# Cutting the tokens of a two-layer decoder step at 256 and 320 columns instead of 288 and 288

## The chip, the cores and the metric

The kernel runs on one core of a Trainium2 chip. The metric is the device time of one execution in microseconds, lower is better. Three runs of the kernel before gave a median of 1583.88 us (1583.41 to 1588.03).

## What is computed

One inference step of two transformer layers with a width of 1024, for 576 tokens: a prompt of 512 tokens and eight samples of eight tokens, all with the same weights. In each layer:

```
mod = silu(c) @ w_ada + b_ada            -> shift, scale and gate, twice
h   = x * (1 + scale1) + shift1
proj = h @ w_in                          (22 column blocks of 128)
   retention, 8 heads (q, k, v, gate)    and sliding-window attention, 8 query heads, 2 kv heads
x   = LN1(alpha * x + gate1 * (concat(ret, swa) @ w_out))
h2  = x * (1 + scale2) + shift2
u   = causal depthwise conv3(h2 @ w_up)  (44 column blocks of 128)
x   = LN2(alpha * x + gate2 * ((silu(u_a) * u_b) @ w_down))
```

The prompt shares one set of modulations; each sample has its own. The outputs are x and the new states of retention, window and convolution.

## The kernel before

Activations lie transposed: 128 features on the partitions, the 576 tokens along the free axis, first the 512 of the prompt, then the 64 of the samples. A product with a 128x128 block of weights therefore has the tokens as its moving columns. A PSUM bank takes 512 of them, so every product is made in two parts, called halves, each of `HA` = 288 columns: the first takes tokens 0 to 287, the second tokens 288 to 575, which are 224 of the prompt and the 64 samples.

Accuracy comes from a split: each weight and each activation is held as two float32r parts, a high and a low one, and `gemm` (L363) makes three matmuls per 128x128 block and half: high by high, high by low, low by high (L369, L370, L371). 96 units of eight blocks per layer, two layers, two halves and three matmuls make 9216 matmuls of 288 columns. Each of them loads its own weights.

`gemm2` (L373) makes both halves of a product one after the other, in two PSUM banks; nearly all products go this way. At three places a layer norm stands between two products, and there the halves are taken apart. `halves` (L928) ends a layer's output product: the first halves of the last four blocks, the second half of one of them, then the statistics and the norm of the first half (`LayerNorm.stats`, L445, `norm`, L460, `make_h`, L243), and then the other three second halves. `skewed` (L915) begins the next product: the first halves of four blocks, with the statistics and norm of the second half put in after the first of them, then the four second halves. This happens after the output projection of both layers and after the down projection of the first. After the last down projection `halves` is followed by the statistics of the second half and `y_out` (L1131), which norms and writes the result.

`stats` uses float32 matmuls against a matrix of constants (L448, L449, L451, L452), then VectorE and ScalarE make 1/sqrt of the variance (L454 to L458, the reciprocal is L457). `norm` is a subtract (L463) and a multiply (L464) for each of the eight feature tiles. `make_h` scales and shifts on ScalarE (L249; the samples on VectorE, L252 and L253), rounds to the high part (L254) and subtracts for the low part (L255, on VectorE or GpSimd).

The program states an order of operations; the tile framework's planner, which works with costs of its own, may put an engine's instructions in another order where the data allow it, so the order on VectorE near the norms isn't the order of the lines.

```
o = half * HA
T.matmul(out[:, 0:HA], lhsT=wh, rhs=xh[:, o:o + HA], start=(k == 0), stop=False)
T.matmul(out[:, 0:HA], lhsT=wh, rhs=xl[:, o:o + HA], start=False, stop=False)
T.matmul(out[:, 0:HA], lhsT=wl, rhs=xh[:, o:o + HA], start=False, stop=(k == n - 1))
```

The functions that the change touches, as they stand:

Of the kernel before, what the change touches and what calls it, by code (L numbers as in the profile page):

```python
# [21 lines left out]
NT = 576  # L22
NP = 512
HA = 288
# [38 lines left out]
def ffn_order():  # L63
    """The feed-forward units: the first pair of the next group goes ahead of a group's down products."""
    seq, done = [], 0
    for g, (f0, f1) in enumerate(GROUPS):
        ahead = f1 + (1 if g + 1 < len(GROUPS) else 0)
        seq += [("up", i) for i in range(done, ahead)] + [("down", g)]
        done = ahead
    return seq  # L70


class Weights:
    """The stream of weight units: 8 tiles of 128x128 each, split exactly into two float32r parts."""
# [41 lines left out]
def _body(ctx, tc, nc, a):  # L116
# [56 lines left out]
    class Ada:  # L173
        """Four (or fewer) 512-wide column blocks of silu(c) @ w_ada + b_ada, one row block of w_ada at a time."""
# [68 lines left out]
    def make_h(src, st, k, half, hi, lo, nm):  # L243
        """h of one feature tile and half of the tokens, split into two float32r parts."""
        s_t, t_t = st
        tmp = tok(f"h{nm}", HA)
        o = half * HA
        n = HA if half == 0 else NP - HA
        S.activation(tmp[:, 0:n], src[:, o:o + n], AF.Identity, bias=t_t[:, k, 0:1], scale=s_t[:, k, 0:1])  # L249
        if half == 1:  # L250
            tv = tmp[:, n:HA].rearrange("p (b t) -> p b t", b=8)
            V.tensor_tensor(tv, src[:, NP:NT].rearrange("p (b t) -> p b t", b=8), bc(s_t[:, k, 1:9], 2, 8), ALU.mult)  # L252
            V.tensor_tensor(tv, tv, bc(t_t[:, k, 1:9], 2, 8), ALU.add)  # L253
        S.copy(hi[:, o:o + HA], tmp[:, 0:HA])  # L254
        (G if k in LO_POOL[half] else V).tensor_tensor(lo[:, o:o + HA], tmp[:, 0:HA], hi[:, o:o + HA].bitcast(F32), ALU.subtract)  # L255

# [4 lines left out]
    # the first modulations, then h  # L261
# [48 lines left out]
    # the bias of the sliding window by distance, by head  # L310
# [52 lines left out]
    def gemm(tiles, X, out, half):  # L363
        n = len(tiles)
        o = half * HA
        for k in range(n):
            wh, wl = tiles[k]
            xh, xl = X[k]
            T.matmul(out[:, 0:HA], lhsT=wh, rhs=xh[:, o:o + HA], start=(k == 0), stop=False)  # L369
            T.matmul(out[:, 0:HA], lhsT=wh, rhs=xl[:, o:o + HA], start=False, stop=False)  # L370
            T.matmul(out[:, 0:HA], lhsT=wl, rhs=xh[:, o:o + HA], start=False, stop=(k == n - 1))  # L371
# [32 lines left out]
    class LayerNorm:  # L404
# [7 lines left out]
        def shift_base(self, m, half, base):  # L412
            """Takes the shift off what the layer's product is added to, once the shift is known."""
            if m > 1:
                o = slice(half * HA, half * HA + HA)
                G.tensor_tensor(base[:, o], base[:, o], self.shift[:, o], ALU.subtract)

        def r_done(self, m, half, tail=False):
            """The sums over the features, of values off by the mean of the first 128 features."""
            o = slice(half * HA, half * HA + HA)  # L420
            x, nm = self.X[m], f"{self.nm}{half}"
            if m == 0:
                ps = psum("tr", f"{nm}mean")
                T.matmul(ps[:, 0:HA], lhsT=ones_h, rhs=x[:, o], start=True, stop=True)
                S.copy(self.shift[:, o], ps[:, 0:HA])
# [7 lines left out]
            if m == 7 and tail:  # L433
                t = self.t7 = tok(f"{nm}s{m}", HA)
# [6 lines left out]
            t = tok(f"{nm}s{m}", HA)  # L441
# [3 lines left out]
        def stats(self, half, tail=False):  # L445
            o, nm = slice(half * HA, half * HA + HA), f"{self.nm}{half}"
            pd, pq = psum("tr", f"{nm}pd"), psum("tr", f"{nm}pq")
            T.matmul(pd[:, 0:HA], lhsT=ones_f, rhs=self.sd[:, o], start=True, stop=not tail)  # L448
            T.matmul(pq[:, 0:HA], lhsT=ones_f, rhs=self.sq[:, o], start=True, stop=not tail)  # L449
            if tail:  # L450
                T.matmul(pd[:, 0:HA], lhsT=ones_f, rhs=self.X[7][:, o], start=False, stop=True)  # L451
                T.matmul(pq[:, 0:HA], lhsT=ones_f, rhs=self.t7, start=False, stop=True)  # L452
            t = tok(f"{nm}var", HA)
            S.activation(t, pd[:, 0:HA], AF.Square)  # L454
            V.tensor_tensor(t, pq[:, 0:HA], t, ALU.subtract)
            S.activation(t, t, AF.Sqrt, bias=eps_ln)
            V.reciprocal(self.rs[:, o], t)  # L457
            S.copy(self.sd[:, o], pd[:, 0:HA])  # L458

        def norm(self, k, half, eng=V, both=False):  # L460
            o = slice(half * HA, half * HA + HA)
# [4 lines left out]
    def add_gated(ps, half, g, m, base, out, nm):  # L466
        """out = base + gate * ps."""
        n = HA if half == 0 else NP - HA
        o = half * HA
        V.scalar_tensor_tensor(out[:, o:o + n], ps[:, 0:n], g[:, m, 0:1], base[:, o:o + n], ALU.mult, ALU.add)  # L470
        if half == 1:
            t = small(f"gs_{nm}", 64)
            V.tensor_tensor(t.rearrange("p (b t) -> p b t", b=8), ps[:, n:HA].rearrange("p (b t) -> p b t", b=8),
# [3 lines left out]
    def attention(l):  # L477
# [18 lines left out]
        kv, svk = [None, None], []  # L496

        def it_kv(s):
            t = kv[s] = unit("S", f"{L}kv{s}")

            def evac(half, ps):
                S.copy(t[:, half * HA:half * HA + HA], ps[:, 0:HA])
# [22 lines left out]
        def it_sq(i):  # L525
            t = sq[i] = unit("X", f"{L}sq{i}", w=NP)

            def evac(half, ps):
                if half == 0:
                    S.mul(t[:, 0:HA], ps[:, 0:HA], 0.125)  # L530
                else:
                    S.mul(t[:, HA:NP], ps[:, 0:NP - HA], 0.125)
                    V.tensor_scalar(qsv[:, :, i, :], ps[:, NP - HA:HA].rearrange("p (b t) -> p b t", b=8), 0.125, None,
# [89 lines left out]
        # the sample group's windows: rows (4 batches, 4 heads, 8 tokens)  # L623
# [65 lines left out]
        def it_kq(i, s):  # L689
# [3 lines left out]
            def evac(half, ps):  # L693
                S.mul(raw[:, half * HA:half * HA + HA], ps[:, 0:HA], sc)
# [20 lines left out]
        def it_v(i):  # L715
            t = vT[i] = unit("X", f"{L}vT{i}")

            def evac(half, ps):
                S.copy(t[:, half * HA:half * HA + HA], ps[:, 0:HA])
# [46 lines left out]
        def ret_states(i):  # L766
            """The states of the prompt after each chunk, and the new ones of the sample group."""
# [30 lines left out]
        def ret_out(i):  # L798
# [23 lines left out]
            # normalise each head  # L822
# [15 lines left out]
        def it_gate(i):  # L838
# [3 lines left out]
            def evac(half, ps):  # L842
                o = half * HA
                S.activation(th[:, o:o + HA], ps[:, 0:HA], AF.Tanh, scale=0.5)
                V.scalar_tensor_tensor(gT[:, o:o + HA], th[:, o:o + HA], 1.0, ps[:, 0:HA], ALU.add, ALU.mult)
# [3 lines left out]
        def gate_out(i):  # L849
            """Back to feature rows, and gated."""  # L850
# [64 lines left out]
    def skewed(items, between):  # L915
        """The first half of the tokens of some products, then the second half of the same ones."""
# [11 lines left out]
    def halves(fn, m0, between):  # L928
        """The last products of a layer by halves, the norm of the first half as soon as it can be had."""
# [13 lines left out]
    for l in range(DEPTH):  # L943
# [68 lines left out]
        def up_evac(t, ps, half):  # L1012
            if half == 0:
                S.copy(t[:, 2:2 + HA], ps[:, 0:HA])
            else:
                n = NP - HA
                S.copy(t[:, 2 + HA:514], ps[:, 0:n])  # L1017
                S.copy(t[:, 514:594].rearrange("p (b t) -> p b t", b=8)[:, :, 2:10],
                       ps[:, n:HA].rearrange("p (b t) -> p b t", b=8))
# [111 lines left out]
        def y_out(half):  # L1131
            o = slice(half * HA, half * HA + HA)
            for k in range(KT):
                ln.norm(k, half, G if k in Y_POOL[half] else V, True)
                if k % 2 == 0:
                    y = tok(f"y{k}{half}", 2 * HA)
                y_k = y[:, k % 2 * HA:k % 2 * HA + HA]
# [172 lines left out]
```

## Time and profile before

| | |
|---|---|
| three runs, median | 1583.88 us |
| profiled execution, span from first to last instruction | 1584.1 us |
| TensorE matmul busy | 96% |
| TensorE weight load busy | 87% |
| VectorE busy | 55% |
| ScalarE busy | 41% |
| GpSimd busy | 31% |
| mean granted TensorE clock | 0.975 of full speed |

The profiled execution has no time of its own beside its span; the span is 0.2 us above the median of the runs. The page's second part cuts the span into 40 slices of 39.6 us and gives each engine's busy share in tenths. In the trace a matmul's record is longer than the distance to the next matmul, because matmuls are pipelined: what a matmul costs in a stream is the distance between two starts, not the duration of one record.

### The profile page before, as it was taken

The numbers are of one execution on the slowest core, as the hardware profiler recorded it, in microseconds if no ns is written. First come the engines' busy times: TensorE is split into PE (matmuls) and PEld (weight loads), VectorE is DVE, ScalarE is ACT, GpSimd is POOL, SyncE is SP. The second block draws the span as 40 slices with busy tenths as digits, with TensorE's granted clock in tenths as the row PEclk, the third lists the DMA queues.
The fourth block names the chain that finished last, engine by engine and source line by source line (L and its number), as shares of the span: only waits on it lengthen the run. The fifth ranks groups of instructions, "written<-read, shape, count | busy, mean of one in ns | idle before, by whom it ended". The sixth has DMA issues, their size and how long they took to land. (4 is left out here: it accounts for less than half of the span.)

```text
span 1584.1 us, 28160 instructions
## 1 busy us (share of the span) xinstructions
PE 1513.1 (96%) x11188; PEld 1382.1 (87%) x11188; DVE 875.5 (55%) x1678; ACT 647.3 (41%) x1318; POOL 498.9 (31%) x647
## 2 busy tenths in 40 slices
PE   7899999997999999999999999999899999999995
PEld 3568778897988888999998788979799999999995
DVE  2236356568655234535576656457876534554577
ACT  1224233335743134415436433333485415523543
POOL 2122122155532122213273222115543313322353
PEclk8999999999999999999999999999999999999997
DMA  9545554223355555232222433233122222223211
GB/s 353 182 151 179 173 178 114 78 85 114 107 173 192 200 189 195 81 92 92 87 67 93 128 87 102 75 97 106 61 80 86 91 80 83 81 81 94 83 57 60
DMA packets 95999, 186.37 MB, mean 118 GB/s; under 512 B 30284, under 2 KB 38524, under 8 KB 95740
## 3 DMA queue, kind: packets, MB, share of 16 engines
q1 hardware_dynamic: 80576, 176.52, 34.9%
q10 hardware_dynamic: 15292, 8.06, 1.8%
q8 instruction: 88, 1.44, 0.4%
q14 instruction: 43, 0.35, 0.1%
HBM read 169.56 MB, written 11.83 MB: 115 GB/s over the span
## 5 line engine op out<-in xcount | busy, mean ns | idle before, releaser
L91 ACT CAST wh<-wr 128x1024 fp32r<-128x1024 f32 x192 | 200.5, 1046 | 308.3 <-PE l0wd02b L370 6.5
L96 POOL TENSOR_TENSOR wl<-wr,wh 128x1024 fp32r<-128x1024 f32 x66 | 158.9, 2407 | 494.6 <-ACT wh L91 417.3
L96 DVE TENSOR_TENSOR wl<-wr,wh 128x1024 fp32r<-128x1024 f32 x126 | 157.7, 1252 | 192.1 <-ACT wh L91 159.2
L190 PE MATMUL ada<-wa,cs 128*32 128x512 f32 x384 | 81.9, 619 | 5.1 <-DVE cs L162 5.1
L1023 POOL COPY l0edge<-l0u 128x2 f32<-128x2 f32 x44 | 37.5, 851 | 127.9 <-ACT l0u L1017 127.9
L1031 DVE SCALAR_TENSOR_TENSOR l0c<-l0u,par,l0c 128x592 f32<-128x592 f32 x44 | 48.2, 1097 | 51.0 <-ACT l0c L1030 48.4
L1023 POOL COPY l1edge<-l1u 128x2 f32<-128x2 f32 x44 | 38.3, 871 | 118.1 <-ACT l1u L1017 118.1
L1031 DVE SCALAR_TENSOR_TENSOR l1c<-l1u,par,l1c 128x592 f32<-128x592 f32 x44 | 48.2, 1098 | 46.3 <-ACT l1c L1030 43.6
L1030 ACT ACTIVATE l0c<-l0u,par 128x592 f32<-128x592 f32 x44 | 38.8, 885 | 4.3 <-POOL l0u L1008 1.0
L1030 ACT ACTIVATE l1c<-l1u,par 128x592 f32<-128x592 f32 x44 | 38.8, 884 | 3.3
L1032 DVE SCALAR_TENSOR_TENSOR l1c<-l1u,par,l1c 128x592 f32<-128x592 f32 x44 | 36.6, 834 | 1.4
L1032 DVE SCALAR_TENSOR_TENSOR l0c<-l0u,par,l0c 128x592 f32<-128x592 f32 x44 | 36.6, 834 | 1.4
L190 PEld LDWEIGHTS ada<-wa,cs 128*32 128x32 f32 x384 | 13.0, 109 | 25.3 <-issue 10.9
L394 ACT CAST l1fhi<-l1c 128x512 fp32r<-128x512 f32 (+1 forms) x44 | 16.8, 430 | 37.7 <-DVE l1c L1037 37.7
L704 POOL TENSOR_TENSOR l1sw<-l1sw,c_sin 128x576 f32<-128x576 f32 x8 | 12.9, 1615 | 56.1 <-DMA l1sw<-l1raw 52.0
L704 POOL TENSOR_TENSOR l0sw<-l0sw,c_sin 128x576 f32<-128x576 f32 x8 | 12.4, 1554 | 54.0 <-DMA l0sw<-l0raw 29.2
L394 ACT CAST l0fhi<-l0c 128x512 fp32r<-128x512 f32 (+1 forms) x44 | 16.9, 431 | 28.5 <-DVE l0c L1037 28.1
L1036 ACT ACTIVATE l0c<-l0c 128x592 f32<-128x592 f32 x22 | 15.4, 699 | 25.8 <-DVE l0c L1032 25.8
L395 DVE TENSOR_TENSOR l1flo<-l1c,l1fhi 128x512 fp32r<-128x512 f32 (+1 forms) x44 | 18.2, 455 | 13.0 <-ACT l1fhi L394 13.0
L395 DVE TENSOR_TENSOR l0flo<-l0c,l0fhi 128x512 fp32r<-128x512 f32 (+1 forms) x44 | 18.2, 455 | 11.7 <-ACT l0fhi L394 11.7
L1008 POOL COPY l0u<-l0edge 128x16 f32<-128x16 f32 x44 | 20.8, 484 | 6.8 <-DMA l0edge<-in_hist 6.8
L1008 POOL COPY l1u<-l1edge 128x16 f32<-128x16 f32 x44 | 21.4, 499 | 0.0
(3207 smaller groups left out, 5986.3 us busy)
## 6 DMA issues: line engine op xcount, KB each, us to landing
wr<-in_wst SPq DMA_DIRECT2D x192, 512.0 KB, 3.6
wa<-in_w_ada SPq DMA_DIRECT2D x192, 256.0 KB, 4.3
x<-in_xT SPq DMA_DIRECT2D x8, 288.0 KB, 5.5
l0sw<-l0raw SPq DMA_DIRECT2D x32, 72.0 KB, 2.0
l0xb<-in_xT SPq DMA_DIRECT2D x8, 288.0 KB, 2.8
x_spill<-l0x ACTq DMA_DIRECT2D x8, 288.0 KB, 3.3
l1sw<-l1raw SPq DMA_DIRECT2D x32, 72.0 KB, 2.0
l1xb<-x_spill SPq DMA_DIRECT2D x8, 288.0 KB, 2.7
```

The source lines that it names most:

```text
L91: nc.scalar.copy(hi, raw)
L96: eng.tensor_tensor(lo, raw, hi.bitcast(F32), ALU.subtract)
L190: T.matmul(self.acc[32 * g:32 * (g + 1), :], lhsT=cs[:, k, :], rhs=self.t[k, g], start=(k == 0), stop=(k == KT - 1))
L394: S.copy(hi, src)
L395: V.tensor_tensor(lo, src, hi.bitcast(F32), ALU.subtract)
L704: G.tensor_tensor(sw, sw, sin_t, ALU.mult)
L1008: G.tensor_copy(t[:, 514:594].rearrange("p (b t) -> p b t", b=8)[:, :, 0:2], hist[mt // 11][:, mt % 11, :].rearrange("p (b t) -> p b t", b=8))
L1023: G.tensor_copy(cm[:, 0:2], t[:, 512:514])
L1030: S.activation(c, t[:, 0:592], AF.Identity, bias=w[3], scale=w[0])
L1031: V.scalar_tensor_tensor(c, t[:, 1:593], w[1], c, ALU.mult, ALU.add)
L1032: V.scalar_tensor_tensor(c, t[:, 2:594], w[2], c, ALU.mult, ALU.add)
L1036: S.activation(ca, ca, AF.Silu)
```

## The change

`HA` is replaced by `CUT` = 256 and `HW` = (256, 320). The first half of every product has 256 columns, the second 320: tokens 256 to 575, which are 256 of the prompt and the 64 samples. Whatever is made by halves follows: the moving operands and PSUM columns of `gemm`, the evacuations, the gated add, the sums and statistics of the layer norm, `make_h`, and the tiles and DMAs of `y_out`. The number of instructions of each kind, their order in the program, the buffers and the loads stay. The rest of the diff deletes comments.

```
-HA = 288
+CUT = 256
+HW = (CUT, NT - CUT)
...
     def make_h(src, st, k, half, hi, lo, nm):
         s_t, t_t = st
-        tmp = tok(f"h{nm}", HA)
-        o = half * HA
-        n = HA if half == 0 else NP - HA
+        w = HW[half]
+        tmp = tok(f"h{nm}", w)
+        o = half * CUT
+        n = w if half == 0 else NP - CUT
...
     def gemm(tiles, X, out, half):
         n = len(tiles)
-        o = half * HA
+        o, w = half * CUT, HW[half]
...
-            T.matmul(out[:, 0:HA], lhsT=wh, rhs=xh[:, o:o + HA], start=(k == 0), stop=False)
-            T.matmul(out[:, 0:HA], lhsT=wh, rhs=xl[:, o:o + HA], start=False, stop=False)
-            T.matmul(out[:, 0:HA], lhsT=wl, rhs=xh[:, o:o + HA], start=False, stop=(k == n - 1))
+            T.matmul(out[:, 0:w], lhsT=wh, rhs=xh[:, o:o + w], start=(k == 0), stop=False)
+            T.matmul(out[:, 0:w], lhsT=wh, rhs=xl[:, o:o + w], start=False, stop=False)
+            T.matmul(out[:, 0:w], lhsT=wl, rhs=xh[:, o:o + w], start=False, stop=(k == n - 1))
...
         def y_out(half):
-            o = slice(half * HA, half * HA + HA)
+            o = slice(half * CUT, half * CUT + HW[half])
...
-                    y = tok(f"y{k}{half}", 2 * HA)
-                y_k = y[:, k % 2 * HA:k % 2 * HA + HA]
+                    y = tok(f"y{k}{half}", 2 * HW[half])
+                y_k = y[:, k % 2 * HW[half]:(k % 2 + 1) * HW[half]]
```

## Rows read from the trace of the kernel before

**Rows 1.** The page: busy time by engine, matmul and clock by slice.
```profile
PE 1513.1 (96%) x11188; PEld 1382.1 (87%) x11188; DVE 875.5 (55%) x1678; ACT 647.3 (41%) x1318; POOL 498.9 (31%) x647
...
PE   7899999997999999999999999999899999999995
...
PEclk8999999999999999999999999999999999999997
```

**Rows 2.** The view of cores: span and mean granted clock.
```profile
core 0: 1584.1 us, clock 0.975
```

**Rows 3.** Stretches: length, each engine's busy time (instructions), clock, DMA share, GB/s.
```profile
349.50:403.00 53.50, 45.26 (x298) 42.63 (x297) 40.14 (x80) 31.89 (x67) 27.76 (x31) 0.94 0.33 106
827.50:866.00 38.50, 33.66 (x222) 31.02 (x220) 31.70 (x73) 25.08 (x52) 16.00 (x12) 0.96 0.23 73
1113.00:1166.30 53.30, 45.30 (x302) 43.19 (x301) 40.32 (x80) 32.21 (x68) 27.68 (x31) 0.94 0.20 64
1562.50:1584.10 21.60, 5.02 (x14) 2.77 (x12) 15.65 (x31) 8.67 (x17) 7.72 (x9) 0.57 0.31 109
403.00:806.00 403.00, 402.89 (x3016) 378.28 (x3015) 203.82 (x302) 167.36 (x306) 120.32 (x194) 1.00 0.43 139
1166.30:1520.00 353.70, 353.70 (x2672) 353.70 (x2671) 186.92 (x254) 160.01 (x289) 107.64 (x180) 1.00 0.28 85
268.40:275.00 6.60, 6.11 (x30) 5.61 (x31) 6.29 (x21) 2.07 (x9) 1.41 (x1) 0.50 0.74 198
1142.10:1145.50 3.40, 3.40 (x14) 3.10 (x13) 2.10 (x4) 1.08 (x3) 2.78 (x3) 0.50 0.38 136
```

**Rows 4.** TensorE in order: start, duration; first matmuls of five successive half products.
```profile
1198.08 0.29 PE L369 MATMUL l1up9a<-l1ghi,wh 128*128 128x288 f32 x1
...
1201.24 0.30 PE L369 MATMUL l1up9b<-l1ghi,wh 128*128 128x288 f32 x1
...
1204.44 0.29 PE L369 MATMUL l1up10a<-l1ghi,wh 128*128 128x288 f32 x1
...
1539.81 0.29 PE L369 MATMUL l1wdl<-l1fhi,wh 128*128 128x288 f32 x1
...
1550.87 0.30 PE L369 MATMUL l1wdl<-l1fhi,wh 128*128 128x288 f32 x1
```

**Rows 5.** TensorE in order at half clock: first and last of 18 matmuls.
```profile
270.73 0.44 PE L369 MATMUL l0rv3b<-h0hi,wh 128*128 128x288 f32 x1
...
274.81 0.42 PE L371 MATMUL l0rv3b<-h0hi,wl 128*128 128x288 f32 x1
```

**Rows 6.** Weight loads in order: two that follow each other after a pause.
```profile
1072.82 0.19 PEld L369 LDWEIGHTS l1wo0a<-l1mshi,wh 128*128 128x128 f32 x1 [0.81 <-issue]
1072.92 0.19 PEld L370 LDWEIGHTS l1wo0a<-l1mslo,wh 128*128 128x128 f32 x1
```

**Rows 7.** Groups of weight loads: busy us, mean ns, idle before.
```profile
L370 PEld LDWEIGHTS l1wdl<-l1flo,wh 128*128 128x128 f32 x56 | 10.5, 188 | 0.1
...
L813 PEld LDWEIGHTS l1o<-l1vk,l1sct 128*128 128x128 f32 x64 | 7.5, 191 | 0.1
```

**Rows 8.** TensorE in order: a run of matmuls with 64 columns.
```profile
1013.21 2.00 PE L813 MATMUL l1o<-l1vk,l1sct 128*128 128x64 f32 x16
```

**Rows 9.** TensorE's waits: tile, line, releaser, us in total, times, longest.
```profile
PE l0a1pd L448 <- DVE l0asd L440: 4.0, 1, 4.0
PE l1a1pd L448 <- DVE l1asd L440: 3.9, 1, 3.9
...
PE l1b1pd L448 <- POOL l1bsd L440: 3.1, 1, 3.1
```

**Rows 10.** VectorE in order near the second layer's first norm.
```profile
1145.75 1.94 DVE L457 RECIPROCAL l1ars<-l1a1var 128x288 f32<-128x288 f32 x1
...
1151.83 0.45 DVE L464 TENSOR_TENSOR l1x<-l1x,l1ars 128x288 f32<-128x288 f32 x1
...
1155.01 0.21 DVE L253 TENSOR_TENSOR h1g<-h1g,st_1t 128x64 f32<-128x64 f32 x1
...
1156.66 0.83 DVE L255 TENSOR_TENSOR l1glo<-h1g,l1ghi 128x288 fp32r<-128x288 f32 x2 [0.32 <-ACT l1ghi L254]
```

**Rows 11.** TensorE in order, same place: statistics, and the first matmul after.
```profile
1141.15 0.75 PE L448 MATMUL l1a1pd<-l1asd,ones_f 128*128 128x288 f32 x2 [3.91 <-DVE l1asd L440]
...
1166.28 0.29 PE L369 MATMUL l1up4a<-l1ghi,wh 128*128 128x288 f32 x1
```

**Rows 12.** TensorE's last instructions.
```profile
1562.90 0.29 PE L371 MATMUL l1wdl<-l1fhi,wl 128*128 128x288 f32 x1
1566.32 1.33 PE L448 MATMUL l1b1pd<-l1bsd,ones_f 128*128 128x288 f32 x2 [3.13 <-POOL l1bsd L440]
1567.44 1.17 PE L449 MATMUL l1b1pq<-l1bsq,ones_f 128*128 128x288 f32 x2
1568.40 1.29 PE L451 MATMUL l1b1pd<-l1x,ones_f 128*128 128x288 f32 x2
```

More of the change, by code (lines that the diff above doesn't have):

```diff
@@ L245, in make_h @@
         s_t, t_t = st
-        tmp = tok(f"h{nm}", HA)
-        o = half * HA
-        n = HA if half == 0 else NP - HA
+        w = HW[half]
+        tmp = tok(f"h{nm}", w)
+        o = half * CUT
+        n = w if half == 0 else NP - CUT
         S.activation(tmp[:, 0:n], src[:, o:o + n], AF.Identity, bias=t_t[:, k, 0:1], scale=s_t[:, k, 0:1])
         if half == 1:
-            tv = tmp[:, n:HA].rearrange("p (b t) -> p b t", b=8)
+            tv = tmp[:, n:w].rearrange("p (b t) -> p b t", b=8)
             V.tensor_tensor(tv, src[:, NP:NT].rearrange("p (b t) -> p b t", b=8), bc(s_t[:, k, 1:9], 2, 8), ALU.mult)
             V.tensor_tensor(tv, tv, bc(t_t[:, k, 1:9], 2, 8), ALU.add)
-        S.copy(hi[:, o:o + HA], tmp[:, 0:HA])
-        (G if k in LO_POOL[half] else V).tensor_tensor(lo[:, o:o + HA], tmp[:, 0:HA], hi[:, o:o + HA].bitcast(F32), ALU.subtract)
+        S.copy(hi[:, o:o + w], tmp)
+        (G if k in LO_POOL[half] else V).tensor_tensor(lo[:, o:o + w], tmp, hi[:, o:o + w].bitcast(F32), ALU.subtract)
     scr = dp.tile([P, 8, 384], F32, name="bias_rows", tag="bias_rows")
@@ L414, in shift_base @@
             if m > 1:
-                o = slice(half * HA, half * HA + HA)
+                o = slice(half * CUT, half * CUT + HW[half])
                 G.tensor_tensor(base[:, o], base[:, o], self.shift[:, o], ALU.subtract)
         def r_done(self, m, half, tail=False):
-            o = slice(half * HA, half * HA + HA)
+            o = slice(half * CUT, half * CUT + HW[half])
             x, nm = self.X[m], f"{self.nm}{half}"
@@ L423, in r_done @@
                 ps = psum("tr", f"{nm}mean")
-                T.matmul(ps[:, 0:HA], lhsT=ones_h, rhs=x[:, o], start=True, stop=True)
-                S.copy(self.shift[:, o], ps[:, 0:HA])
+                T.matmul(ps[:, 0:HW[half]], lhsT=ones_h, rhs=x[:, o], start=True, stop=True)
+                S.copy(self.shift[:, o], ps[:, 0:HW[half]])
             if m < 2:
@@ L433, in r_done @@
             if m == 7 and tail:
-                t = self.t7 = tok(f"{nm}s{m}", HA)
+                t = self.t7 = tok(f"{nm}s{m}", HW[half])
                 S.activation(t, x[:, o], AF.Square)
@@ L440, in r_done @@
                 (V if m == 7 else G).tensor_tensor(self.sd[:, o], self.sd[:, o], x[:, o], ALU.add)
-            t = tok(f"{nm}s{m}", HA)
+            t = tok(f"{nm}s{m}", HW[half])
             S.activation(t, x[:, o], AF.Square)
@@ L445, in stats @@
         def stats(self, half, tail=False):
-            o, nm = slice(half * HA, half * HA + HA), f"{self.nm}{half}"
+            o, nm, w = slice(half * CUT, half * CUT + HW[half]), f"{self.nm}{half}", HW[half]
             pd, pq = psum("tr", f"{nm}pd"), psum("tr", f"{nm}pq")
-            T.matmul(pd[:, 0:HA], lhsT=ones_f, rhs=self.sd[:, o], start=True, stop=not tail)
-            T.matmul(pq[:, 0:HA], lhsT=ones_f, rhs=self.sq[:, o], start=True, stop=not tail)
+            T.matmul(pd[:, 0:w], lhsT=ones_f, rhs=self.sd[:, o], start=True, stop=not tail)
+            T.matmul(pq[:, 0:w], lhsT=ones_f, rhs=self.sq[:, o], start=True, stop=not tail)
             if tail:
[L451 to L455, printed above, removed]
+                T.matmul(pd[:, 0:w], lhsT=ones_f, rhs=self.X[7][:, o], start=False, stop=True)
+                T.matmul(pq[:, 0:w], lhsT=ones_f, rhs=self.t7, start=False, stop=True)
+            t = tok(f"{nm}var", w)
+            S.activation(t, pd[:, 0:w], AF.Square)
+            V.tensor_tensor(t, pq[:, 0:w], t, ALU.subtract)
             S.activation(t, t, AF.Sqrt, bias=eps_ln)
             V.reciprocal(self.rs[:, o], t)
-            S.copy(self.sd[:, o], pd[:, 0:HA])
+            S.copy(self.sd[:, o], pd[:, 0:w])
         def norm(self, k, half, eng=V, both=False):
-            o = slice(half * HA, half * HA + HA)
+            o = slice(half * CUT, half * CUT + HW[half])
             x = self.X[k]
@@ L466, in add_gated @@
     def add_gated(ps, half, g, m, base, out, nm):
-        n = HA if half == 0 else NP - HA
-        o = half * HA
+        n = CUT if half == 0 else NP - CUT
+        o = half * CUT
         V.scalar_tensor_tensor(out[:, o:o + n], ps[:, 0:n], g[:, m, 0:1], base[:, o:o + n], ALU.mult, ALU.add)
@@ L472, in add_gated @@
             t = small(f"gs_{nm}", 64)
-            V.tensor_tensor(t.rearrange("p (b t) -> p b t", b=8), ps[:, n:HA].rearrange("p (b t) -> p b t", b=8),
+            V.tensor_tensor(t.rearrange("p (b t) -> p b t", b=8), ps[:, n:HW[1]].rearrange("p (b t) -> p b t", b=8),
                             bc(g[:, m, 1:9], 2, 8), ALU.mult)
@@ L501, in evac @@
             def evac(half, ps):
-                S.copy(t[:, half * HA:half * HA + HA], ps[:, 0:HA])
+                S.copy(t[:, half * CUT:half * CUT + HW[half]], ps[:, 0:HW[half]])
             def done():
@@ L529, in evac @@
                 if half == 0:
-                    S.mul(t[:, 0:HA], ps[:, 0:HA], 0.125)
+                    S.mul(t[:, 0:CUT], ps[:, 0:CUT], 0.125)
                 else:
-                    S.mul(t[:, HA:NP], ps[:, 0:NP - HA], 0.125)
-                    V.tensor_scalar(qsv[:, :, i, :], ps[:, NP - HA:HA].rearrange("p (b t) -> p b t", b=8), 0.125, None,
+                    S.mul(t[:, CUT:NP], ps[:, 0:NP - CUT], 0.125)
+                    V.tensor_scalar(qsv[:, :, i, :], ps[:, NP - CUT:HW[1]].rearrange("p (b t) -> p b t", b=8), 0.125, None,
                                     ALU.mult)
@@ L693, in evac @@
             def evac(half, ps):
-                S.mul(raw[:, half * HA:half * HA + HA], ps[:, 0:HA], sc)
+                S.mul(raw[:, half * CUT:half * CUT + HW[half]], ps[:, 0:HW[half]], sc)
             return item(U_KQ[s][i], f"{L}r{i}{s}", evac, lambda: rotate(i, s, raw))
@@ L718, in evac @@
             def evac(half, ps):
-                S.copy(t[:, half * HA:half * HA + HA], ps[:, 0:HA])
+                S.copy(t[:, half * CUT:half * CUT + HW[half]], ps[:, 0:HW[half]])
             return item(U_V[i], f"{L}rv{i}", evac)
@@ L842, in evac @@
             def evac(half, ps):
-                o = half * HA
-                S.activation(th[:, o:o + HA], ps[:, 0:HA], AF.Tanh, scale=0.5)
-                V.scalar_tensor_tensor(gT[:, o:o + HA], th[:, o:o + HA], 1.0, ps[:, 0:HA], ALU.add, ALU.mult)
+                o, w = half * CUT, HW[half]
+                S.activation(th[:, o:o + w], ps[:, 0:w], AF.Tanh, scale=0.5)
+                V.scalar_tensor_tensor(gT[:, o:o + w], th[:, o:o + w], 1.0, ps[:, 0:w], ALU.add, ALU.mult)
             return item(U_G[i], f"{L}rg{i}", evac)
@@ L1013, in up_evac @@
             if half == 0:
-                S.copy(t[:, 2:2 + HA], ps[:, 0:HA])
+                S.copy(t[:, 2:2 + CUT], ps[:, 0:CUT])
             else:
-                n = NP - HA
-                S.copy(t[:, 2 + HA:514], ps[:, 0:n])
+                n = NP - CUT
+                S.copy(t[:, 2 + CUT:514], ps[:, 0:n])
                 S.copy(t[:, 514:594].rearrange("p (b t) -> p b t", b=8)[:, :, 2:10],
-                       ps[:, n:HA].rearrange("p (b t) -> p b t", b=8))
+                       ps[:, n:HW[1]].rearrange("p (b t) -> p b t", b=8))
         def conv(t, mt):
@@ L1131, in y_out @@
         def y_out(half):
-            o = slice(half * HA, half * HA + HA)
+            o = slice(half * CUT, half * CUT + HW[half])
             for k in range(KT):
```

## Prediction

> **What bounds the kernel now.** I read the page first: TensorE is busy in nearly every slice, no other engine in much over half of the time, and the clock is full but for the first and last slices [rows 1]. The view of stretches says where that holds. From 403 to 806 us and from 1166 to 1520 us the matmul row is busy without a gap, while VectorE is busy for half of the time and ScalarE for less [rows 3]: there the time is the number of matmuls times the distance of their starts, and evacuations, gated adds and transfers lie beside them. TensorE falls short in four places: three changeovers, where a layer norm stands between two products (349.5 to 403, 827.5 to 866 and 1113 to 1166 us, of which 8.2, 4.8 and 8.0 us aren't busy), and the end, where 21.6 us hold 5.0 us of matmuls [rows 3].
>
> So the first question is what a float32r matmul costs in a stream as a function of its columns. The records' durations can't say it; the order of TensorE can. 24 matmuls of a first half go from 1198.08 to 1201.24 us, 131.7 ns each; the 24 of the second half from there to 1204.44 us, 133.3 ns each; 84 first-half matmuls from 1539.81 to 1550.87 us, 131.7 ns each again [rows 4]. At the lower level of the clock, 1.2 GHz, 17 distances take 4.08 us, 240 ns each [rows 5, 3].
>
> At 1.2 GHz 240 ns is 288 columns at one per cycle, with nothing left over. At 2.4 GHz the columns would take 120 ns, and there are 11.7 ns more in the first half and 13.3 ns more in the second. I read this as a stage in front of the array that doesn't slow with the array's clock: it needs 131.7 to 133.3 ns for 288 columns, which hides below 240 ns and shows above 120 ns. Is that stage the weight load? Two loads that don't wait follow each other after 0.10 us [rows 6], and 16 matmuls of 64 columns with 128x128 weights take 2.00 us together with the last one's run-out, at most 125 ns each, and about 111 ns if a run-out of 0.3 us is taken off [rows 8]. A load's record is as long beside a stream as without one, 188 against 191 ns [rows 7]. So a load needs about 111 ns, less than the distance in a stream. And both halves load the same weights, while their distances differ: the stage handles the moving operand.
>
> **The change, part by part.**
>
> *Matmuls.* 9216 matmuls of 288 columns become 4608 of 256 and 4608 of 320; a pair has 576 columns as before. Where the clock is at 1.2 GHz nothing changes (240 + 240 against 213.3 + 266.7 ns). That is 2 x (1 - 0.975) = 5% of the span [rows 2]; it leaves 4378 pairs at the upper level. A pair now takes 131.7 + 133.3 = 265.0 ns [rows 4]. If the excess is a fixed amount for each matmul, or a share of its columns, the pair is the same up to the question which excess each half has. The two halves differ in one thing that the stage can see, the start of the moving operand: tiles are 576 float32 = 2304 bytes apart, a first half starts at 0 of its tile and a second at 1152 bytes. Since 2304 is 9 x 256, first halves start at every multiple of 256 bytes relative to each other and yet all show 131.7 ns; a second half is off by 128 bytes. After the change it starts at 1024 bytes, a multiple of 256: as a first half does. So I give both the smaller excess: 106.7 + 11.7 = 118.3 ns and 133.3 + 11.7 = 145.0 ns, together 263.3 ns, 1.67 ns less a pair. 4378 x 1.67 ns = 7.3 us gained. The bounds: none if the second half keeps its excess, and 7.3 us lost if both halves get 13.3 ns. I take the gain, because an equal start is the nearest row, but it isn't certain. The 256-column matmul stays above the load's 111 ns, with 7 ns to spare.
>
> The Trainium skill, TensorE: Matmul & The Clock Gate, section on the back-to-back issue gap, gives a distance of the columns over 2.4 GHz plus 2.5 ns, which would be 122.5 ns for 288 columns. The trace has 131.7 and 133.3 ns and so disagrees; the page's rule is for one number of columns at a time and says nothing of float32r. With it the new pair would be 109.2 + 135.8 = 245.0 ns, and this is the first rival's case below.
>
> *VectorE, ScalarE, GpSimd in the dense stretches.* The same instructions with 32 columns fewer in first halves and 32 more in second ones; nothing in sum, and under TensorE's full row [rows 3]. Were that cover gone they would still sum to nothing.
>
> *The end.* Everything after the last product at 1562.90 us works on the second half [rows 12], so 32 columns are added to each step of that path. The price of a column on VectorE: (0.45 - 0.21) us / 224 = 1.07 ns, 34 ns for 32 columns [rows 10]. Eight float32 records at 1.2 GHz, two in 0.96 us at 288 columns, become 1/9 longer: 4 x 0.107 = 0.43 us [rows 12]. The reciprocal, 1.94 us, gains at most 1/9, 0.2 us [rows 10]. Some 14 VectorE steps of the norm by 34 ns make 0.5 us, and ScalarE and GpSimd before and between them some 0.2 us. Together 1.3 us lost (bounds 0.8 and 2).
>
> *The three changeovers.* The last four first halves before a norm take 96 x 13.3 ns = 1.3 us less, and the one second half made before the statistics 0.3 us more: the first half's statistics start 1.0 us earlier. The first half's norm has some 21 VectorE steps and a reciprocal with 32 columns fewer: 0.9 us faster. So VectorE, which TensorE waits for here (3.9 us at the second half's statistics, 4.0 us in the first layer [rows 9]), comes to those statistics some 1.7 us earlier. From there to the last tile of the second half, 1141.15 to 1157.5 us [rows 10, 11], every step has 32 columns more: 19 VectorE steps, a reciprocal, and float32 matmuls of which a part runs at 1.2 GHz [rows 3], 1.2 us in all. TensorE then still has 8.8 us of second-half products, to 1166.28 us [rows 11], 66 matmuls that grow by 11.7 ns: 0.8 us. Net, 0.3 to 0.4 us lost each time. The first halves of the next product save 1.3 us too, but where TensorE waits anyway, so I count nothing for it. The bounds for each are 1 us gained (if a saving on the first half reaches the end) and 4 us lost (the third rival). I take 0.4, together 1.2 us.
>
> *What else moves.* No instruction, queue entry or wait is added. The transfers of the result keep their count, with rows of 1024 and 1280 bytes instead of 1152. The planner may choose another order near the norms, since its costs change with the sizes; this is in the changeovers' bounds.
>
> **Sum.** 1584.1 - 7.3 + 1.3 + 1.2 = 1579.3 us for an execution like the profiled one, which is 0.2 us above the median of the runs: 1579.1, I say 1579. Below, a change of 0.3%, 4.75 us, is about the least that a measurement of this kernel tells from none: under 1579.1 us is faster, over 1588.6 us slower. The forecast lies on the first edge; the gain from the start address decides.
>
> **Rivals.**
>
> 1. *The excess belongs to 288 and vanishes.* If 11.7 ns come from a width that isn't a multiple of 64, 256 and 320 columns would stream bare: 111 ns (the load's bound) + 133.3 = 244.3 ns, 20.7 ns less a pair, 4378 x 20.7 ns = 91 us, less 2.5 us lost elsewhere: 1496 us. For: 133.3 ns is just 320 columns at 2.4 GHz, as if 288 were rounded up. Against: 131.7 ns is less than 320 columns can take, and all first halves have it. By the page named above, with 135.8 ns for 320 columns, it would be some 11 us more than that.
>
> 2. *A floor.* If the 131.7 ns are a least distance of float32r matmuls with their own weights, not a price of columns, 256 columns still take 131.7 ns and 320 take 145: 276.7 ns, 11.7 ns more a pair, 51 us more, with the 2.5 us: 1638 us. For: the trace has one width in this type, so it shows no slope. Against: the loads follow each other in 0.10 us [rows 6], and the halves differ by their moving operand alone.
>
> 3. *The changeovers lose more* (the other side). The place is the second half's chain from statistics to the last low part; the mechanism, that TensorE's cover shrinks while the chain grows. Cover: 1.3 us less of first-half products. Chain: 1.2 us more. TensorE then has more idle time, and one more stretch like the one from 1142.1 to 1145.5 us, 3.4 us at clock 0.50 [rows 3], would cost 1.7 us. That makes 4.2 us for each changeover, 12.6 us, with the end 13.9 us: 1590.7 us if the pitch gains its 7.3 us, 1598 us if not. It makes the kernel slower than before from 2 us lost in each changeover on (7.3 - 1.3 = 6.0 us in three), and measurably so from 3.6 us. For: idle time and half clock stand there already [rows 3, 9]. Against: VectorE gets 1.7 us of it back by its shorter first half.
>
> **How the numbers follow.** The forecast has 0.65, with 0.30 below 1579.1 us, 0.31 within and 0.04 above 1588.6 us (its own range is 1573 to 1592). Rival 1 has 0.12, all faster. Rival 2 has 0.06, all slower. Rival 3 has 0.17, of which 0.04 within and 0.13 slower. Faster 0.42, same 0.35, slower 0.23. A range from 1571 to 1600 us holds the forecast and rival 3, 0.8; the bounds of the terms (7.3 us either way for the pitch, 4 us lost for each changeover) set its ends.
>
> **What would show it.** In the order of TensorE, first halves of 24 matmuls at 118.3 ns and second halves at 145.0 ns bear the main term out; 120 and 146.7 say that the start address doesn't matter; 111 and 133 are rival 1, 131.7 and 145 rival 2. The dense stretches must stay dense. After the last product, the end must take 22.9 us where it took 21.6. In each changeover, from the last matmul of the output product to the first one after the skewed products, some 0.4 us more; 4 us more and a longer time at clock 0.50 would be rival 3. The prediction is wrong if the sum of a pair leaves 263 to 267 ns, or if the changeovers move by more than 2 us each.

## The result, and the profile after

The changed kernel is slower: 1596.5 us in the median of four runs (1595.8 to 1599.2), where the kernel before took 1584.5 us (four runs, 1583.4 to 1588.0). The ratio is 1.0068, 95% interval 1.0048 to 1.0087. The profiled execution, the longest of the four, spans 1597.4 us, 13.3 more than the one before.

The page after, its busy times and TensorE's slices:

```profile
PE 1521.7 (95%) x11188; PEld 1390.3 (87%) x11188; DVE 874.5 (55%) x1678; ACT 647.2 (41%) x1318; POOL 497.6 (31%) x647
...
PE   7899999997999999999998999999799999999995
...
PEclk8999999898999999999999999989899999999998
```

Against [rows 1] no engine but TensorE has more work; TensorE's busy time grows by 8.6 us with the same instructions. Where, the stretches show (columns as in [rows 3]): three changeovers, the end, the two dense stretches, and one in the attention of layer 0.

```profile
354.50:408.80 54.30, 45.16 (x292) 42.91 (x291) 40.35 (x80) 32.67 (x68) 28.15 (x31) 0.91 0.34 107
835.60:875.30 39.70, 34.96 (x218) 32.23 (x217) 31.35 (x72) 25.13 (x52) 15.31 (x12) 0.91 0.24 73
1122.70:1177.00 54.30, 45.14 (x292) 42.98 (x292) 40.11 (x79) 32.92 (x68) 27.90 (x31) 0.91 0.21 64
1575.70:1597.40 21.70, 4.67 (x12) 2.61 (x11) 15.58 (x29) 8.69 (x17) 7.25 (x7) 0.64 0.31 109
409.10:814.70 405.60, 405.44 (x3018) 380.25 (x3017) 203.41 (x301) 166.64 (x303) 121.37 (x195) 1.00 0.43 137
1177.00:1552.80 375.80, 375.64 (x2813) 375.21 (x2813) 200.66 (x280) 165.56 (x300) 123.02 (x195) 1.00 0.27 83
262.30:300.00 37.70, 33.27 (x253) 27.71 (x253) 20.02 (x65) 16.45 (x53) 6.18 (x7) 0.82 0.32 92
```

The dense stretches are still dense at full clock, and longer (the first takes 405.7 us; 403.3 before from the same first to the same last product). Each of the outer changeovers is 54.3 us long with 45.2 or 45.1 busy: 9.1 and 9.2 us idle where [rows 3] had 8.2 and 8.0. The reason for the dense part is in TensorE's order, which answers to [rows 4]:

```profile
1208.96 0.28 PE L371 MATMUL l1up9a<-l1ghi,wh 128*128 128x256 f32 x1
...
1211.84 0.31 PE L371 MATMUL l1up9b<-l1ghi,wh 128*128 128x320 f32 x1
...
1215.37 0.28 PE L371 MATMUL l1up10a<-l1ghi,wh 128*128 128x256 f32 x1
```

24 matmuls of 256 columns take 2.88 us, 120.0 ns each, and 24 of 320 take 3.53 us, 147.1 ns. Over many products the medians are 119.9 and 146.8 ns, 266.7 ns a pair. Both halves have the larger excess, some 13.3 ns, that only the second half had before. TensorE's waits, as in [rows 9]:

```profile
PE l0a1pd L450 <- DVE l0asd L442: 4.6, 1, 4.6
PE l1a1pd L450 <- DVE l1asd L442: 4.6, 1, 4.6
...
PE l1b1pd L450 <- POOL l1bsd L442: 2.2, 1, 2.2
PE l1up0h L372 <- POOL l1glo L257: 1.9, 1, 1.9
...
PE l1up0h L372 <- DVE l1glo L257: 1.7, 2, 1.5
```

And TensorE at the first of the four output products before the norm, at the statistics of the second half, at the first product behind the changeover, and at its last product, as in [rows 11, 12]:

```profile
1110.28 0.28 PE L371 MATMUL l1wo<-l1mshi,wh 128*128 128x256 f32 x1
...
1149.22 0.90 PE L450 MATMUL l1a1pd<-l1asd,ones_f 128*128 128x320 f32 x1 [4.64 <-DVE l1asd L442]
...
1176.96 0.28 PE L371 MATMUL l1up4a<-l1ghi,wh 128*128 128x256 f32 x1
...
1575.95 0.31 PE L373 MATMUL l1wdl<-l1fhi,wl 128*128 128x320 f32 x1
1578.43 1.38 PE L450 MATMUL l1b1pd<-l1bsd,ones_f 128*128 128x320 f32 x2 [2.17 <-POOL l1bsd L442]
```

A table by stage, for all full kernels that were profiled: how much longer each stage is than in the first profile of before. It is worked out from the starts of the same named matmul in both orders, always the first one of a first half, since the start of a second half moves with the cut itself. "Dense" is both layers' feed-forward products and the first output products; "again" is a second profile of the same kernel.

| us | start | attention 0 | attention 1 | dense | changeovers 1, 2, 3 | end | span |
|---|---|---|---|---|---|---|---|
| after (256) | +1.2 | +3.9 | -0.2 | +5.0 | +0.6, +1.3, +1.2 | +0.3 | +13.3 |
| after, again | +0.6 | 0.0 | +0.5 | +5.1 | +0.6, +1.1, +1.2 | +0.3 | +9.3 |
| before, again | +0.8 | +0.8 | -2.0 | +0.1 | -0.7, 0.0, 0.0 | 0.0 | -1.0 |
| 256 outside the changeovers | +0.1 | +1.8 | +5.8 | +5.0 | -0.7, 0.0, 0.0 | 0.0 | +11.9 |
| 256 in the changeovers | -0.1 | 0.0 | -0.6 | 0.0 | +0.5, +1.7, +1.2 | 0.0 | +2.7 |
| 320 | +0.1 | -0.6 | +4.8 | +4.8 | -0.3, +3.2, -1.9 | -0.2 | +9.8 |
| 304 | +0.8 | -1.7 | -1.5 | -9.5 | +2.3, +1.6, +3.0 | -0.3 | -5.4 |
| 304 outside the changeovers | +0.2 | -1.9 | +1.6 | -9.3 | -0.2, 0.0, 0.0 | 0.0 | -9.6 |
| 276 | +0.4 | +0.6 | +2.8 | -8.3 | -0.2, -0.1, +0.5 | -0.1 | -4.4 |
| 276 outside the changeovers | +0.5 | -1.2 | -0.4 | -8.4 | -0.7, 0.0, 0.0 | 0.0 | -10.2 |
| 288 with a gap | -2.4 | -2.2 | +1.8 | -1.6 | -0.5, +0.2, -0.1 | -0.1 | -4.9 |

The dense part, the third changeover and the end repeat within 0.1 us; the start and the attention move by up to 4 us between two executions of one kernel.

### The profile page after: what moved, and what is told of

It is laid out like the page before. It is cut to its first block, busy times and chain, and to the rows that moved or that the text cites. A ratio compares the mean times of both kernels' runs of the same rounds, so it can differ in the third digit from the quotient of the medians.

```text
span 1597.4 us, 28160 instructions
## 1 busy us (share of the span) xinstructions
PE 1521.7 (95%) x11188; PEld 1390.3 (87%) x11188; DVE 874.5 (55%) x1678; ACT 647.2 (41%) x1318; POOL 497.6 (31%) x647
## 5 line engine op out<-in xcount | busy, mean ns | idle before, releaser
L397 DVE TENSOR_TENSOR l0flo<-l0c,l0fhi 128x512 fp32r<-128x512 f32 (+1 forms) x44 | 18.2, 454 | 11.7 <-ACT l0fhi L396 11.7
L1038 ACT ACTIVATE l1c<-l1c 128x592 f32<-128x592 f32 x22 | 15.4, 700 | 20.1 <-DVE l1c L1034 20.1
```

## Experiments

**Streams by column count and place.** Streams of 48 matmuls, no evacuation:

```
+    def stream(name, s, n, groups=2, o=0):
+        ps = pp.tile([P, 512], F32, tag="ps", name=name, bufs=8)
...
+                T.matmul(ps[:, o:o + n], lhsT=wh[:, w], rhs=xh[:, s:s + n], start=(k == 0), stop=False)
+                T.matmul(ps[:, o:o + n], lhsT=wh[:, w], rhs=xl[:, s:s + n], start=False, stop=False)
+                T.matmul(ps[:, o:o + n], lhsT=wl[:, w], rhs=xh[:, s:s + n], start=False, stop=(k == 7))
```

> The step is left out whole; only streams of 48 matmuls run, with the kernel's pattern (high weights on high part, high weights on low part, low weights on high part), one stream for each pair of a column count and a start column of the moving operand, whose tiles begin at the same place modulo 256 bytes as the kernel's. Place theory: the fixed excess of a matmul over its columns at 2.4 GHz depends on where the operand lies. Then 288 columns give 131.7 ns a matmul from column 0 and 133.3 ns from column 288 here too, some other start columns change it between these two, and 256 columns have a start at which they take 118.3 ns instead of 120.0. Role theory: the smaller excess belongs to the first half of a product (fresh weights, another PSUM tile), not to its place. Then every start column gives 288 columns the same pitch in these streams. Both expect 256 columns from column 0 at 120.0 ns, 320 from column 256 at 146.7 ns, and a line through the counts: columns / 2.4 + 11.7 to 13.3 ns.

TensorE's order in that kernel, the first matmul of each stream: 256 columns from column 0, 8, 16 and 24; 320 columns from 0 and 8; 288 columns from 128, 256, 288 and 320, and the stream behind them.

```profile
102.41 0.28 PE L103 MATMUL n256s<-xh,wh 128*128 128x256 f32 x1
...
108.16 0.28 PE L103 MATMUL n256s<-xh,wh 128*128 128x256 f32 x1
...
113.82 0.28 PE L103 MATMUL n256s<-xh,wh 128*128 128x256 f32 x1
...
119.48 0.28 PE L103 MATMUL n256s<-xh,wh 128*128 128x256 f32 x1
...
153.70 0.31 PE L103 MATMUL n320s<-xh,wh 128*128 128x320 f32 x1
...
160.74 0.31 PE L103 MATMUL n320s<-xh,wh 128*128 128x320 f32 x1
...
217.06 0.29 PE L103 MATMUL n288s<-xh,wh 128*128 128x288 f32 x1
...
223.38 0.29 PE L103 MATMUL n288s<-xh,wh 128*128 128x288 f32 x1
...
229.70 0.30 PE L103 MATMUL n288s<-xh,wh 128*128 128x288 f32 x1
...
236.10 0.29 PE L103 MATMUL n288s<-xh,wh 128*128 128x288 f32 x1
...
242.42 0.31 PE L103 MATMUL n320s<-xh,wh 128*128 128x320 f32 x1
```

The distance of two such starts over 48 is the pitch. 288 columns: 131.7, 131.7, 133.3 (from column 288), 131.7 ns. Of nine more starts, 0, 16, 24 and 64 give 131.5 to 131.8 and 8, 32, 40, 48, 56 give 133.2 to 133.4. The column decides, not the half: the place theory holds. The place of the result is no matter: from PSUM columns 16, 32, 64 and 128 the pitch is 131.6 or 131.7 ns. 256 columns: 119.8 from 0, but 117.9 from 8 and 16. 320 columns: 146.5 to 146.8 from all ten starts tried. So the rule "a start at a multiple of 256 bytes has the smaller excess" is true of 288 columns (0, 64, 128, 256, 320), though 16 and 24, which are no such starts, have it too, and it is false of 256 and 320. The line through the counts that both theories expected isn't there either: from column 0, 264 columns took 120.0 ns, hardly more than 256, and 284 took 133.0.

**The changeovers apart.** The cut is set when code is emitted, one for the products whose halves follow each other at once (the attention's, too) and one for the changeovers and the end:

```
+def cut(n):
+    global CUT, HW
+    CUT, HW = n, (n, NT - n)
...
+            cut(CUT_DENSE)    # proj, the wo loop, up_pair, the wd loop
...
+        cut(CUT_CHANGE)    # skewed, halves and what follows them
```

256 outside, 288 in the changeovers:

> Only the products whose halves follow each other at once (all but those of the changeovers and the end) are cut at 256; the changeovers and the end stay at 288. Additive theory: it pays the dearer pair of matmuls, 1.6 ns x some 3730 pairs = +6.0 us, and the longer half clock in the attention of layer 0, +3.4 us, but not the +3.1 us of the three changeovers: 1593 to 1595 us. Rival (the changeovers start the loss and the rest follows from them, the clock above all): within 5 us of before, 1584 to 1589 us.

1596.1 us; ratio 1.0052 (1.0033 to 1.0070); the rival falls. And the reverse:

> The reverse: only the changeovers and the end (halves in separate loops, the statistics, the norms, the outputs) are cut at 256; every other product stays at 288. Additive theory: +3.1 us at the changeovers, +0.3 us at the end and 648 dearer pairs in them of which the +3.1 us already holds the cost: 1587 to 1589 us. Rival: most of the loss is here, 1592 us or more.

1589.5 us; ratio 1.0019 (1.0009 to 1.0030); here, too, the rival falls. The kernel before took 1586.9 us in these runs, 2.4 more than in those of the result; with that allowed for, both kernels are near what was expected. +0.52% and +0.19% sum to 0.71%, and the whole change has 0.68%: the parts are additive, and about three quarters of the loss come from outside the changeovers.

**The cut mirrored** (`CUT = 320`).

> The whole cut mirrored: 320 columns first, then 256. Additive theory: the pair of matmuls costs the same 266.7 ns as with 256 first, +6.6 us over all pairs, and the changeovers differ by which half is long: with 320 columns the first half's norm on VectorE is longer but the cover from the second half's first product is shorter: 1590 to 1597 us. Rival (256 first loses because its short half covers too little, and 320 first gains that back): 1587 us or less.

1597.3 us, at the upper edge of what was expected, and the rival falls; ratio 1.0064 (1.0046 to 1.0082). The pair is again 266.7 ns (146.8 and 119.9), dense +4.8 us. The order of the halves is no matter for the pitch.

**Pairs by cut and shift.** The same streams for pairs of halves.

> The step is left out again; streams of 48 matmuls, two for each cut c of the 576 columns and each shift b of the operand's tile by b columns: c columns from column b, and 576 - c from column b + c. From the streams before: 304 from 0 at 138.0 and 272 from 304 at 123.4 make the pair 261.3 ns, where 288 and 288 make 265.0 and 256 and 320 make 266.5. Place theory: the sum differs from cut to cut and from shift to shift by up to 5 ns, with the same total of columns, and 288 / 288 is one of the dearer pairs. Rival (the 123.4 ns was a flaw of one stream, since 272 from column 0 took 125.2): no pair below 264 ns.

Unshifted pairs ran from 259.1 ns (276) over 261.2 (304) to 267.2 (300); 304 from column 0 took 137.7 ns and 272 from 304 took 123.5, as before. The place theory stands and the rival falls, but no simple rule comes out: the excess over columns / 2.4 lies between 8 and 17 ns.

**Cut at 304** (`CUT = 304`), everywhere and then outside the changeovers only:

> The whole cut at 304: 304 columns first, then 272. Place theory: the pair costs 261.3 ns in place of 265.0, -3.7 ns x 4378 pairs = -16 us, and the changeovers lie between those of 288 (0) and of 320 (about +1 us): 15 us faster than before, ratio 0.990 to 0.992. In the dense stretch of feed-forward units after the first changeover the pair of half products shrinks by 24 x 3.7 ns = 0.09 us. Rival (any uneven cut costs what 256 and 320 cost, since the second half's place is not what decides in the kernel): ratio 1.004 or more.

1581.8 us; ratio 0.9971 (0.9958 to 0.9984). TensorE's order:

```profile
1197.39 0.30 PE L371 MATMUL l1up9a<-l1ghi,wh 128*128 128x304 f32 x1
...
1200.69 0.29 PE L371 MATMUL l1up9b<-l1ghi,wh 128*128 128x272 f32 x1
...
1203.65 0.30 PE L371 MATMUL l1up10a<-l1ghi,wh 128*128 128x304 f32 x1
```

6.26 us for 24 pairs, 261 ns: the pitch carried over, the dense part gives 9.5 us. But the changeovers lose 7 us, so I expected too much.

> 304 in the dense products, 288 in the changeovers and at the end. In the run with 304 everywhere the three changeovers took +2.3, +1.7 and +3.0 us more than before. Additive theory: this run is faster than that one by these 7 us, less the pitch gain of some 650 pairs x 3.3 ns = 2 us that the changeovers then forgo: ratio 0.993 to 0.995. Rival (the dearer changeovers of 304 are half-clock stretches that fall now here, now there): ratio 0.997, as with 304 everywhere.

1576.5 us; ratio 0.9941 (0.9926 to 0.9957), as expected: the changeovers are back at -0.2, 0 and 0 us, and this is one of the two fastest kernels of the study, some 9 us faster than before and 20 faster than the changed one by the ratios.

**Cut at 276**, outside the changeovers and then everywhere:

> Only the products whose halves follow each other at once are cut at 276, the changeovers and the end stay at 288. Place theory: the streams gave 125.7 ns for 276 columns from 0 and 133.4 ns for 300 from 276, a pair of 259.1 ns against 265.0: -5.9 ns x some 3730 pairs = -22 us, ratio 0.985 to 0.988. Rival (a column count's pitch in the streams does not carry over, the kernel's tiles alternate in another order): ratio 0.995 or more.

1576.0 us; ratio 0.9944 (0.9931 to 0.9958).

> The whole cut at 276. Place theory: -5.9 ns x 4378 pairs = -26 us, and at the changeovers something between nothing (288) and +2.8 us (256): ratio 0.983 to 0.986, the changeovers no dearer than in the run with 288 there. Rival (any cut off 288 costs some 2 us a changeover, as 304 did): ratio 0.986 to 0.990, not better than 276 in the dense products alone.

1579.0 us; ratio 0.9960 (0.9945 to 0.9975). Both are faster, both by less than a half of what I expected. In the kernel 276 columns take 128.4 ns (125.7 in the streams), 300 take 134.2: 262.5 ns a pair. The streams didn't predict the kernel at this cut, and the rival of the first of the two, that a stream's pitch doesn't carry over, comes nearest. Why isn't shown: the streams read two tiles, 4096 bytes apart, where the kernel reads many tiles of 2304 bytes in turn, and the kernel has other engines at work beside TensorE; neither was tried by itself.

**Second profiles.**

> The changed kernel once more, unedited, for a second profile. Steady theory: what the first profile showed repeats, +3.9 us and 13.7 us at half clock between the first query product and the first output product of layer 0, +1.2 us before it. Rival (that part is where half-clock stretches happen to fall in one execution): it differs by 2 us or more from the first profile, while the dense stretches repeat within 0.1 us (404.3 and 375.9 us long) and the changeovers within 0.3 us.

> The kernel before once more, unedited, for a second profile. Steady theory: 6.8 us and 17.1 us at half clock in the attention of the two layers, as in the first. Rival: other sums, by one stretch of 3.4 us or more, and the attention's length with them; the dense stretches repeat within 0.1 us (403.3 and 373.5 us from the first product after the changeover to the first of the last four).

(404.3 is a slip: the first profile after has 405.7 us there.) The dense stretches are 405.7 and 375.9 us again, and 403.4 and 373.5 for before. But the attention of layer 0 takes 3.9 us less than in the first profile of the changed kernel: here the rival holds. The same 253 matmuls as in the row of 262.30, and the half-clock stretch of the first changeover, in the second profile:

```profile
262.20:295.50 33.30, 28.88 (x253) 24.02 (x253) 20.11 (x65) 16.23 (x53) 6.18 (x7) 0.95 0.37 104
372.90:383.10 10.20, 6.21 (x23) 5.42 (x24) 7.33 (x9) 2.05 (x5) 6.66 (x7) 0.50 0.46 154
```

They take 33.3 us instead of 37.7, and the clock is 0.95 instead of 0.82. The stretches at half clock in the attention are not fixed by the kernel; the one of 10.2 us in the changeover is in both.

**288 with a gap.** The same counts as before, with the second half of h moved to a place that is a multiple of 256 bytes:

```
+GAP = 32
-        return [(unit("H", f"{nm}hi{k}", F32R), unit("H", f"{nm}lo{k}", F32R)) for k in range(KT)]
+        return [(unit("H", f"{nm}hi{k}", F32R, NT + GAP), unit("H", f"{nm}lo{k}", F32R, NT + GAP)) for k in range(KT)]
...
-        o = half * HA
+        o = half * (X[0][0].shape[1] - HA)
```

> 288 and 288 as before, but the tiles of h are 608 columns wide and their second half lies at columns 320 to 607, a multiple of 256 bytes from the tile's start; the 32 columns between are never read (two small tiles of the attention have one buffer in place of two to make room, and the first h is split in two pieces). The operands of the output and down products stay as they were. Place theory: second halves of the products of h go from 133.4 to 131.7 ns with the same 288 columns, an up product pair from 265.1 to 263.5 ns, a down product's stays at 265; some 3000 pairs x 1.6 ns = 4.9 us faster, ratio 0.996 to 0.998. Rival (the second half pays for being the second, its other PSUM tile or the change of half): pair 265.1 ns and no change of the time.

1581.2 us; ratio 0.9974 (0.9962 to 0.9986). TensorE's order:

```profile
1193.78 0.29 PE L373 MATMUL l1up9a<-l1ghi,wh 128*128 128x288 f32 x1
...
1196.95 0.29 PE L373 MATMUL l1up9b<-l1ghi,wh 128*128 128x288 f32 x1
...
1200.12 0.29 PE L373 MATMUL l1up10a<-l1ghi,wh 128*128 128x288 f32 x1
```

Both halves now take 3.17 us, 132.1 ns: the rival falls, the second half pays nothing for being second. But 131.7 was expected, and the pair is 264.5, not 263.5: tiles are now 2432 bytes apart, so they begin at two places modulo 256, and the first half got 0.5 ns dearer. Of the 4.9 us in the profile only 1.6 are in the dense part; 4.6 came before the output products, 2.4 of them at the start, where the first h was made in two pieces. The time agrees with the expectation, the reason mostly doesn't.

## Why the prediction was wrong

**The failed step is the start address**: "So I give both the smaller excess: 106.7 + 11.7 = 118.3 ns and 133.3 + 11.7 = 145.0 ns, together 263.3 ns". Measured: 120.0 and 146.7, 266.7 ns. Over the forecast's 4378 pairs that is 7 us lost where 7.3 were forecast as gained, 14 us between them, against 17.5 us between forecast and result. The bound "7.3 us lost if both halves get 13.3 ns" was the right value. I had two rows, both of 288 columns, and drew a rule from them for counts that no row showed. The streams show that start and count decide together, and that 288 from column 0 was a favoured pair of the two. I had written that 120 and 146.7 ns would say that the start doesn't matter; they came, and it does matter, for 288 columns and for 256. My signs of being wrong (a pair outside 263 to 267 ns, a changeover off by more than 2 us) were too wide: neither came, since those bounds held the gain and the loss alike. The forecast that the second half's excess follows the place of its operand was right for 288 columns, in the streams and, less cleanly, in the kernel with the gap.

**Affine pitch, rivals 1 and 2.** Right for these counts: an excess of 11.7 to 13.3 ns over the columns, no vanishing at multiples of 64 and no floor at 131.7 ns. At half clock nothing is left over, as I had it: the median distances in the changed kernel are 213 and 267 ns. A floor exists lower down: 224 and 240 columns both took 112 ns a matmul in the streams and 64 columns 110 ns, close to the 111 ns estimated for a weight load from [rows 8] (2.00 - 0.3 us over 15 distances make 113). The Trainium skill, TensorE: Matmul & The Clock Gate, section Back-to-back issue gap, says that weight load and matmul together set the spacing of a stream; the floor fits that, at 110 to 112 ns for float32r where the page gives about 81 ns for 128 columns of a type that it doesn't name. The distance that the prediction took from that section is given there for a matmul by itself and not for such a stream.

The prediction had also worked out 109.2, 122.5 and 135.8 ns for 256, 288 and 320 columns, and set the 122.5 against the measured 131.7 and 133.3. The run with the streams by column count had four more of another type, bf16, again 48 matmuls each and a weight load for every matmul. Their first matmuls:

```profile
461.75 0.28 PE L111 MATMUL bf<-bx,bw 128*128 128x256 bf16 x1
...
467.00 0.53 PE L111 MATMUL bf<-bx,bw 128*128 128x288 bf16 x3
...
472.88 0.57 PE L111 MATMUL bf<-bx,bw 128*128 128x320 bf16 x3
...
479.40 0.38 PE L111 MATMUL bf<-bx,bw 128*128 128x512 bf16 x1
```

That is 109.4, 122.5 and 135.8 ns, the prediction's distances in bf16, and float32r takes 9 to 11 ns more from column 0 in the same run. So they do hold in a stream here, for that type.

**The changeovers** (forecast +0.4 each) took +0.9, +1.2 and +1.2 us, in the mean of two profiles of either kernel: rival 3's place, at a quarter of its price. TensorE waits there for VectorE at the statistics of the second half, so what it does or loses ahead of them costs nothing by itself. The third changeover from the statistics to the first dense product, before and after:

```profile
1141.15:1166.28 25.13, 24.08 (x163) 23.43 (x164) 15.28 (x39) 17.87 (x39) 9.68 (x18) 0.93 0.19 61
...
1149.22:1176.96 27.74, 26.91 (x171) 25.75 (x172) 16.36 (x39) 19.09 (x39) 10.22 (x18) 0.89 0.18 58
```

Up to the statistics, from the first of the four output products, it is 1.4 us shorter (1149.22 - 1110.28 against 1141.15 - 1100.80), where I had 1.7. From there on it is 27.7 us instead of 25.1, +2.6, where I had +2.0, and all of that is busy time: 2.8 us more busy, 0.2 less idle. By estimate three things make most of it, and no run parts them. TensorE has eight matmuls more left, since the planner put the statistics behind 25 of the next product's matmuls instead of 33, in every kernel with 256 at the changeovers: 1.0 us at 120 ns. The 96 second halves take 13.4 ns more each, 1.3 us, and the first halves behind the statistics give 0.7 back. And half clock fills some 6 us of it where it filled 3.4: by [rows 4, 5], where a pair takes 480 ns instead of 265, an estimate of 1.2 us, which I had in rival 3 and not in the forecast. The stretch at half clock is 10.2 us long, in place of two of 3.4, in those same kernels; what of it lies ahead of the statistics is hidden in TensorE's wait, and so are the 1.5 us for VectorE's low parts, a wait that I didn't have. The whole changeover therefore has 57.5 us of busy time before and after, and 9.2 us idle instead of 8.0, though its price isn't paid where it is idle. With 276 the statistics come 0.5 us earlier and the rest takes 1.0 us longer; with 304 1.4 earlier and 4.4 longer, at a clock of 0.86.

**The end** (forecast +1.3) took +0.3. After the last product TensorE waits 2.2 us instead of 3.1 [rows 12]. A likely cause, which no run isolates: the 84 second-half matmuls before it take some 1.1 us longer (84 x 13.4 ns), so GpSimd's sums lag less. With 256 in the changeovers and at the end alone, the end was as long as before.

**What the forecast left out.** In the mean of two profiles each, the changed kernel is 11.8 us longer. Dense +5.0, changeovers +3.3 and the end +0.3 leave 3.2 us for the start and the attention. Some 960 pairs there at 1.6 ns are 1.5 us; the other 1.7 us are within what two executions of one kernel differ by, and stay open. 256 outside the changeovers lost 7.6 us in the attention of its one profile and 8 us in all by its ratio, so the attention may lose more than its pitch; no run settles that.

## What to carry to other kernels

In a stream that TensorE bounds, a matmul's pitch is to be measured for each count and place of the operand that a change brings in; two rows of one count give no rule for another. Here 5.5 ns in 265, a pair of 266.7 against one of 261.2 ns, were most of the 1.3% between the changed kernel and the one with 304 in the dense products. A cut that is best for the dense stream need not be best for the stages where a norm must catch up: here 304 and 272 in the dense products with 288 and 288 at the changeovers beat both cuts used throughout. Before a difference in a stage with many short waits is explained, the same kernel is to be profiled twice.

## Not expected of the hardware

The excess of a float32r matmul over columns / 2.4 GHz isn't a constant: from 8 to 17 ns in the streams of 256 to 320 columns. It changes with four columns more (280 from column 0 took 127.7 ns, 284 took 133.2: 11.1 and 14.9 ns over the columns) and with a start 8 columns further on. At half clock the least distance nearly doubles: streams of 128 and 160 columns took 213.8 and 213.9 ns a matmul, where 224 columns at full clock took 111.9. And TensorE fell to half clock in a stream without any wait: after 5.3 us of 64-column matmuls, which were issued every 110 ns, the streams of 96 to 160 columns ran at 1.2 GHz:

```profile
262.00:267.00 5.00, 5.00 (x48) 5.00 (x46) 0.00 (x0) 0.00 (x0) 1.00 0.00 0
267.20:297.50 30.30, 30.30 (x146) 30.30 (x146) 0.00 (x0) 0.00 (x0) 0.51 0.00 1
```
